# Cutting the first half of an output projection into pieces between attention steps, and splitting the first head's weights on another engine

## The chip, the core and the metric

The kernel runs on one core of a Trainium2 chip. TensorE (PE in the profile) multiplies matrices and transposes tiles; VectorE (DVE), ScalarE (ACT) and GpSimd (POOL) work element by element; transfers are issued by SyncE (SP) and by ScalarE. Each engine takes its instructions in the order in which they were built, and waits on semaphores for the others. The metric is the device time of one execution in microseconds. Before the change it is 2502.75 us, the median of three runs (2502.54 to 2502.87).

## The reference

Two transformer layers over 1024 tokens of width 1024, in float32. Layer 0 mixes tokens by differential attention (8 heads, each with two softmax maps whose difference weighs the values), layer 1 by latent attention (16 heads). After each stands a gated MLP with a causal convolution of width 3.

```python
def diff_attention(h, w_qkv, lq1, lk1, lq2, lk2, subln_g, w_o, lambda_init, cos, sin):
    qkv = h @ w_qkv
    ...
    def block(args):
        sc = jnp.einsum('bqhcd,bkhcd->bhcqk', qb, k).astype(jnp.float32) * scale
        p = masked_softmax(sc, chunk_mask(blk, s)[None, None, None])
        a = p[:, :, 0] - lam * p[:, :, 1]
        return jnp.einsum('bhqk,bkhe->bqhe', a.astype(v.dtype), v)
    ...
    o = rms_norm(o, subln_g) * (1.0 - lambda_init)
    return o.reshape(b, s, D_MODEL) @ w_o

for i in range(DEPTH):
    h = rms_norm(x, attn_norm_g[i])
    x = x + (diff_attention(h, ...) if i % 2 == 0 else mla_attention(h, ...))
    h = rms_norm(x, ffn_norm_g[i])
    x = x + conv_ffn(h, ...)
return rms_norm(x, final_norm_g)
```

## The kernel before, in words

**Float32 products in three passes.** Every operand of a matrix product is split into a rounded high part and the rest, the low part: `hi` (line 127, a cast on ScalarE) and `lo` (line 130, the source minus its high part, on VectorE or GpSimd). `mm3` (lines 119 to 121) then multiplies low by high, high by high and high by low into one accumulator in PSUM. A 128x512 accumulator over four blocks of 128 takes 12 matmuls, one over eight blocks takes 24.

**The PSUM banks.** `big()` gives one of two tiles of 1024 columns, named S; `bank("b")` one of three tiles of 512 columns, named b; `bank("u")` the one tile of 512 columns named u. A new accumulator in u can begin only when the last one has been read out.

**The start of layer 0.** Eight token tiles of 128 rows are fetched. `token_tile` takes each through a sum of squares (line 157, ScalarE), `root` (line 162 on VectorE, line 163 on GpSimd), the norm (line 349, VectorE, two operands in SBUF) and eight transposes on TensorE (line 182), whose results are split by ScalarE and VectorE into H. The projections of head 0 (`unit(0, which, half)`, which = 1 for k, 0 for q, 2 for v) multiply H by the head's weights; `split_w` splits those weights (slots s8 to s11), the low part on GpSimd. A k or q unit ends with `rope`: a copy of the accumulator (line 233, ScalarE), a shuffle of it (line 234, VectorE), and three steps on GpSimd (lines 235 to 237), then the splits into k (lines 430, 431) or into q (lines 127, 125 and, on GpSimd, 130). A v unit ends with a copy (line 417) and transposes of that copy.

**The head steps.** `steps` runs 32 steps of `DaStep` (eight heads, four steps each) in a software pipeline: scores of step t, transposes and product of step t-1, and the finish of step t-2; between them stand the projection units of the next head. In step t, `scores` fills two S tiles for each of two query blocks; DVE takes the row maximum, ScalarE the exponentials, GpSimd a scaling (line 149), DVE the difference of the two maps (line 1356). `turn` (line 249) transposes the result, `product` multiplies by v in bank b. Every second step ends with `finish`: two matmuls against ones (lines 1384, 1385), three ScalarE steps, one GpSimd step (line 173), three VectorE steps, and a store of 128x512 results to o_d in DRAM (line 1389, issued by SP).

**Output projection 0.** `project_first` computes, for the eight token tiles in the order 0, 4, 1, 5, 2, 6, 3, 7, the contribution of heads 0 to 3 and adds the input x: it loads o_d (line 449, SP), splits it into four pieces of slot s12 (high on ScalarE, low on GpSimd), multiplies, and adds to X in slots s8 to s11. The first four tiles accumulate in u, in two halves of 512 columns, with an addition for each half (line 473); the last four in S, with one addition of 1024 columns (line 478). `project_rest` does heads 4 to 7 in S, adds (line 554), stores x (line 555), normalises (line 515), forms sums on GpSimd (lines 492 to 499) and transposes them (line 182) for the MLP. The output projection of layer 1 uses the same two functions, with all tiles of the first half in S.

**What sets the order.** A list scheduler orders the instructions of each engine by its own estimate of time; only inside a region that is marked as manual (from `project_rest` to the end of each MLP) do PE and DVE instructions keep the order of the code among themselves. Instructions written ahead of the region may be set between those inside it. So a change in the code can move rows on every engine, and the order that results is fixed in the program.

Of the kernel before, what the change touches and what calls it, by code (L numbers as in the profile page):

```python
# [18 lines left out]
P = 128  # L19
S = 1024  # L20
D = 1024
NT = S // P
# [34 lines left out]
class Trunk:  # L57
# [220 lines left out]
    def steps(self, attend, units, prepare, n):  # L278


        steps = []
        for t in range(n + 2):
            now = before = None
            u = []
            if t < n:
                now = attend(t)
                steps.append(now)
                prepare(t)
                u = units(t)
# [12 lines left out]
            if now:  # L302
                now.weigh(1)
            if t >= 2:
                steps[t - 2].finish()


    def diff_attention(self, o_d, prefetch):
        nc, a = self.nc, self.a

        H = [[[self.at(f"s{4 * half + 2 * part + g}", [P, 4, 512], F32R) for g in range(2)] for half in range(2)] for part in range(2)]
# [18 lines left out]
            if h < DA_HEADS:  # L330
                raws[h, which] = self.fetch(a["da_wqkv"][h, which], D)

        def split_w(h, which):
            if h < DA_HEADS:
                raw = raws.pop((h, which))
                w = self.w([P, 2, D], F32R)
                self.hi(w[:, 0, :], raw)
                self.lo(w[:, 1, :], raw, w[:, 0, :], nc.gpsimd)
                heads[h]["w", which] = w[:, 0, :], w[:, 1, :]


# [12 lines left out]
        def unit(h, which, half):  # L354
            hd = heads[h]
            return self.da_unit(R, H, hd["w", which], which, half, hd, tab)

        xs = [fetch_x(0)]
        g = self.gain("s11", a["attn_norm_g"][0])
# [2 lines left out]
        xs += [fetch_x(3)]  # L362
        fetch_w(0, 0)
        nc.sync.dma_start(tab, a["rope_da"])
        split_w(0, 1)
        for i in range(4):
            token_tile(i, xs[i])
            if i == 1:
                self.load_constants()
        xs += [fetch_x(4), fetch_x(5), fetch_x(6)]  # L370
        fetch_w(0, 2)
        split_w(0, 0)
        self.run([unit(0, 1, 0)])
        split_w(0, 2)
        fetch_w(1, 1)
        self.run([unit(0, 0, 0)])
        for i in range(4, NT):
            if i + 3 < NT:
                xs += [fetch_x(i + 3)]
            token_tile(i, xs[i])  # L380
        self.run([unit(0, 2, 0)])

        def prepare(t):
            h, p = divmod(t, 4)
            if p == 0:
# [12 lines left out]
        def units(t):  # L398
            h, p = divmod(t, 4)
            todo = [[(h, 1, 1), (h, 2, 1)], [(h, 0, 1), (h + 1, 1, 0)], [(h + 1, 0, 0)], [(h + 1, 2, 0)]][p]  # L400
            return [unit(*u) for u in todo if u[0] < DA_HEADS]

        self.steps(lambda t: DaStep(self, R, *divmod(t, 4), heads, o_d), units, prepare, 4 * DA_HEADS)

    def da_unit(self, R, H, W, which, half, hd, tab):

        nc = self.nc
        acc = self.bank("u")
        for k in range(KD):
            wh, wl = (w[:, k * P : (k + 1) * P] for w in W)  # L410
            rh, rl = (H[part][half][k // 4][:, k % 4, :] for part in range(2))
            self.mm3(acc, wh, wl, rh, rl, k == 0, k == KD - 1)
            if k == 3:
                yield
        if which == 2:
            v = R.rope([P, 512])
            nc.scalar.copy(v, acc)
# [39 lines left out]

        return into

    def project_first(self, W, o_d, os, x_src, at, early):  # L460

        nc = self.nc
        X = [None] * NT
        for q, pair in enumerate(self.PAIRS):
            for i in pair:
                X[i] = at(q, i)
                nc.sync.dma_start(X[i], x_src[i * P : (i + 1) * P, :])
                into = self.project(i, range(0, 4), W, o_d, os, self.raw)
                if q < early:
                    for b in (0, 512):  # L470
                        y = self.bank("u")
                        into(y, b)
                        nc.vector.tensor_add(X[i][:, b : b + 512], X[i][:, b : b + 512], y)
                else:
                    y = self.big()
                    for b in (0, 512):
                        into(y[:, b : b + 512], b)
                    nc.vector.tensor_add(X[i], X[i], y)
        return X

    def project_rest(self, W, o_d, os, X, at, x_d, g, junk, places, nat, more):

# [704 lines left out]
    def mla_heads(self, cT, kT, v_d, o_d):  # L1187
# [85 lines left out]
        def units(t):  # L1273
            p, u = divmod(t, 8)

            at = (2, 3, 4, 5, 6, 7) if p == 0 else (0, 1, 3, 4, 5, 7)
            return [pair_units(p + 1)[i]() for i in range(6) if at[i] == u and p + 1 < pairs]

        def attend(t):

# [163 lines left out]
def kernel_body(tc, a, out):  # L1444
    with ExitStack() as ctx:
# [41 lines left out]

        W = []
        step, finish = prefetcher(a["da_w_o"], W, slots(*range(8)))
        k.diff_attention(o_d[0], step)  # L1490
        finish()
        first = {}
# [86 lines left out]
        heads.rest(step)  # L1579
        finish()  # L1580
        places = iter(units(2, 3, 4, 5, 12, 13, 10, 11))
        X = k.project_first(W, o_d[1], k.ring(*halves(0, 1, 2, 3)), x_d[1], lambda q, i: k.at(next(places), [P, D]), 0)
# [114 lines left out]
```

## Time and profile before

| | |
|---|---|
| median of three runs | 2502.75 us |
| the profiled execution | 2506.9 us |
| its span | 2505.1 us |
| TensorE busy | 2390.0 us, 95% of the span |
| VectorE, ScalarE, GpSimd busy | 1979.3, 1271.8, 725.4 us |
| mean granted TensorE clock | 0.988 |

A timeline row reads: start in the span, duration, engine, line, operation, tile written and tiles read, shape, count, and in brackets the idle time of the engine ahead of it with what ended it. A row of the table of stretches gives for each engine the busy time and the number of instructions, then the granted TensorE clock as a share of full speed, the DMA share and GB/s. A row of the list of waits gives the total, the number of times and the longest. Tile names are given without their numbers: s, u and h are slots in SBUF, S, b and u (as a matmul's output) the banks.

### The profile page before, as it was taken

How to read it: one execution, taken by the hardware profiler on the slowest of the kernel's cores; microseconds unless marked ns; L12 is line 12 of the kernel's file. 1: busy time of each engine (PE TensorE's matmuls, PEld its weight loads, DVE VectorE, ACT ScalarE, POOL GpSimd, SP SyncE). 2: the span in 40 equal slices, each digit the busy share in tenths (PEclk: the TensorE clock that was granted, in tenths of full speed). 3: DMA queues.
4: the chain of work that ended last, by engine and by line, in shares of the span. 5: the costliest groups of instructions: out<-in, count | busy, mean ns of one | idle time of the engine just before them, and what ended most of it. 6: DMA issues, size and time to landing. Idle time of an engine off the chain costs nothing.

```text
span 2505.1 us, 32665 instructions
## 1 busy us (share of the span) xinstructions
PE 2390.0 (95%) x11960; PEld 2015.0 (80%) x11960; DVE 1979.3 (79%) x3164; ACT 1271.8 (51%) x2323; POOL 725.4 (29%) x562
## 2 busy tenths in 40 slices
PE   6999999889999999999989899999999999999998
PEld 5787877778888888878878788888887888887887
DVE  6788888765788888889973787877368888888998
ACT  5566666643444444444443777777244444444444
POOL 5666666534300000000041566666350000000002
PEclk9999999989999999999999999999999999999999
DMA  4111111313122222454121211113322222227401
GB/s 148 35 46 35 36 41 43 109 58 124 65 79 85 85 84 85 151 192 145 57 107 43 80 37 39 39 55 98 107 97 76 93 76 84 86 83 272 154 20 76
DMA packets 95104, 214.44 MB, mean 86 GB/s; under 512 B 8640, under 2 KB 33856, under 8 KB 94784
## 3 DMA queue, kind: packets, MB, share of 16 engines
q1 hardware_dynamic: 86048, 185.09, 22.3%
q10 hardware_dynamic: 8896, 27.27, 3.0%
q8 instruction: 94, 1.54, 0.2%
q14 instruction: 66, 0.54, 0.1%
HBM read 159.89 MB, written 52.43 MB: 85 GB/s over the span
## 4 chain that ended last, share of the span: by engine, by line
PE 75%; DVE 13%; ACT 4%; issue 3%; DMA 3%; POOL 2%; SPq 0%; DVEq 0%; ACTq 0%; POOLq 0%
PE S L119 12%; PE S L120 12%; PE S L121 12%; PE b L119 7%; PE b L120 7%; PE b L121 7%; PE u L119 3%; PE u L120 3%; PE u L121 3%; PE b L249 2%; DVE s L130 2%; PE b L182 1%; PE u L1433 1%; PE u L1432 1%; DVE u L1356 1%
## 5 line engine op out<-in xcount | busy, mean ns | idle before, releaser
L119 PE MATMUL S<-s,u 128*128 128x512 f32 (+1 forms) x752 | 285.8, 380 | 5.6 <-DVE u L769 3.8
L121 PE MATMUL S<-s,u 128*128 128x512 f32 (+1 forms) x752 | 284.1, 378 | 0.0
L120 PE MATMUL S<-s,u 128*128 128x512 f32 (+1 forms) x752 | 284.1, 378 | 0.0
L127 ACT CAST u<-h 128x512 fp32r<-128x512 f32 (+2 forms) x210 | 126.4, 620 | 284.4 <-DVE h L631 255.9
L163 POOL TENSOR_TENSOR st<-st,mhalf 128x1 f32<-128x1 f32 x56 | 41.3, 740 | 717.5 <-DVE st L162 709.9
L119 PE MATMUL b<-s,u 128*128 128x512 f32 x588 | 231.5, 394 | 0.5
L120 PE MATMUL b<-s,u 128*128 128x512 f32 x588 | 229.6, 390 | 0.0
L121 PE MATMUL b<-s,u 128*128 128x512 f32 x588 | 229.5, 390 | 0.0
L679 DVE SCALAR_TENSOR_TENSOR u<-u,conv,u 128x1023 f32<-128x1023 f32 (+1 forms) x176 | 225.0, 1278 | 1.6 <-ACT u L675 1.6
L149 POOL TENSOR_TENSOR u<-u,st 128x384 f32<-128x384 f32 (+7 forms) x160 | 171.6, 1080 | 136.0 <-DVE st L1418 102.9
L119 PE MATMUL u<-s,s 128*128 128x512 f32 x432 | 177.6, 411 | 17.9 <-DVE h L234 12.8
L130 POOL TENSOR_TENSOR u<-s,u 128x960 fp32r<-128x960 f32 (+1 forms) x5 | 12.8, 2576 | 598.8 <-DVE s L130 587.6
L130 DVE TENSOR_TENSOR u<-b,u 128x512 fp32r<-128x512 f32 (+1 forms) x256 | 158.1, 631 | 32.6 <-ACT u L127 30.7
L127 ACT CAST s<-u 128x512 fp32r<-128x512 f32 (+2 forms) x195 | 128.1, 692 | 100.6 <-PE u L121 32.5
L121 PE MATMUL u<-s,s 128*128 128x512 f32 x432 | 173.7, 402 | 0.0
L120 PE MATMUL u<-s,s 128*128 128x512 f32 x432 | 173.0, 400 | 0.0
L119 PEld LDWEIGHTS S<-s,u 128*128 128x128 f32 x752 | 141.4, 188 | 34.2 <-issue 4.4
L121 PEld LDWEIGHTS S<-s,u 128*128 128x128 f32 x752 | 141.3, 188 | 26.3
L120 PEld LDWEIGHTS S<-s,u 128*128 128x128 f32 x752 | 141.4, 188 | 26.0
L127 ACT CAST u<-b 128x512 fp32r<-128x512 f32 (+1 forms) x256 | 133.7, 551 | 51.6 <-PE b L249 43.0
L249 PE MATMUL b<-ident,u 128*128 128x128 f32 x864 | 137.3, 279 | 13.6 <-DVE u L130 5.7
L682 ACT ACTIVATE u<-u 128x1024 f32<-128x1024 f32 x44 | 46.7, 1062 | 199.1 <-DVE u L679 199.1
(260 smaller groups left out, 6885.4 us busy)
## 6 DMA issues: line engine op xcount, KB each, us to landing
u<-in_ffn_up SPq DMA_DIRECT2D x88, 512.0 KB, 3.9
g_d<-u ACTq DMA_DIRECT2D x44, 512.0 KB, 2.6
u<-in_ffn_down SPq DMA_DIRECT2D x66, 256.0 KB, 5.2
u<-g_d SPq DMA_DIRECT2D x62, 256.0 KB, 4.3
s<-in_da_wqkv SPq DMA_DIRECT2D x24, 512.0 KB, 3.6
x_d<-u SPq DMA_DIRECT2D x16, 512.0 KB, 2.9
s<-x_d SPq DMA_DIRECT2D x8, 1024.0 KB, 11.0
u<-o_d SPq DMA_DIRECT2D x24, 256.0 KB, 2.8
```

What stands on the lines that cost most here:

```text
L119: mm(out, lh, rl, start=first, stop=False, skip_group_check=onto)
L120: mm(out, lh, rh, start=False, stop=False, skip_group_check=onto)
L121: mm(out, ll, rh, start=False, stop=last, skip_group_check=onto)
L127: self.nc.scalar.copy(out, src)
L130: (eng or self.nc.vector).tensor_sub(out, src, hi.bitcast(F32))
L149: self.nc.gpsimd.tensor_mul(x, x, s.to_broadcast(list(x.shape)))
L163: nc.gpsimd.tensor_tensor(r, s, self.mhalf, ALU.pow)
L182: self.nc.tensor.transpose(ps[:, k * P : (k + 1) * P], src[:, k * P : (k + 1) * P], self.ident)
L249: self.nc.tensor.transpose(ps[:, j * P : (j + 1) * P], probs[t][:, k : k + P], self.ident)
L679: nc.vector.scalar_tensor_tensor(t[half][:, back:], u[half][:, : S - back], w, t[half][:, back:], ALU.mult, ALU.add)
L682: nc.scalar.activation(t[0], t[0], AF.Silu)
L1356: nc.vector.scalar_tensor_tensor(p0, p1, w, p0, ALU.mult, ALU.add)
```

## The change

It has three parts.

1. **The start.** The low parts of head 0's three weight tiles are computed on VectorE instead of GpSimd. The first split (`split_w(0, 1)`) comes after two token tiles; the fifth token tile is taken right after the k unit and the sixth before the v unit. The q unit `unit(0, 0, 0)` accumulates in a b bank instead of u. `load_constants` comes later.
2. **The end of attention 0.** `project_first` becomes a generator of pieces. Its pieces are handed to the steps 30 to 33 as units, two tiles to each, so that they stand between the last head's steps in the code; the o_d tiles are loaded into h8 and h9 instead of s13; all eight tiles accumulate in u, a half of 512 columns at a time. The prefetch of the projection's weights begins one step earlier.
3. **Output projection 1** uses the same pieces with bank b: two halves of 512 columns and two additions a tile, instead of S and one addition.

```diff
@@ steps
-            u = []
             if t < n:
                 now = attend(t)
                 steps.append(now)
                 prepare(t)
-                u = units(t)
+            u = units(t)
+            if now:
                 now.scores(0)
@@ diff_attention
-        def split_w(h, which):
+        def split_w(h, which, eng=nc.gpsimd):
...
-                self.lo(w[:, 1, :], raw, w[:, 0, :], nc.gpsimd)
+                self.lo(w[:, 1, :], raw, w[:, 0, :], eng)
...
-        split_w(0, 1)
         for i in range(4):
+            if i == 2:
+                split_w(0, 1, nc.vector)
             token_tile(i, xs[i])
-            if i == 1:
-                self.load_constants()
...
-        split_w(0, 0)
+        split_w(0, 0, nc.vector)
         self.run([unit(0, 1, 0)])
-        split_w(0, 2)
+        token_tile(4, xs[4])
+        split_w(0, 2, nc.vector)
         fetch_w(1, 1)
-        self.run([unit(0, 0, 0)])
-        for i in range(4, NT):
-            if i + 3 < NT:
-                xs += [fetch_x(i + 3)]
+        self.run([unit(0, 0, 0, "b")])
+        self.load_constants()
+        for i in range(5, NT):
+            if i + 2 < NT:
+                xs += [fetch_x(i + 2)]
             token_tile(i, xs[i])
-        self.run([unit(0, 2, 0)])
+            if i == 5:
+                self.run([unit(0, 2, 0)])
...
-            if h + 1 == DA_HEADS:
+            if t >= 4 * DA_HEADS - 5:
                 prefetch()
...
         def units(t):
             h, p = divmod(t, 4)
+            if t >= 4 * DA_HEADS - 2:
+                if not ready:
+                    ready.append(project(self.ring("h8", "h9")))
+                return [next(ready[0]) for _ in range(2)]
@@ project_first
+        def tile(i, into):
+            for b in (0, 512):
+                y = bank()
+                into(y, b)
+                nc.vector.tensor_add(X[i][:, b : b + 512], X[i][:, b : b + 512], y)
+                yield
...
-                into = self.project(i, range(0, 4), W, o_d, os, self.raw)
-                if q < early:
-                    for b in (0, 512):
-                        y = self.bank("u")
-                        into(y, b)
-                        nc.vector.tensor_add(X[i][:, b : b + 512], X[i][:, b : b + 512], y)
-                else:
-                    y = self.big()
-                    for b in (0, 512):
-                        into(y[:, b : b + 512], b)
-                    nc.vector.tensor_add(X[i], X[i], y)
-        return X
+                yield tile(i, self.project(i, range(0, 4), W, o_d, os, raw))
@@ kernel_body
-        X = k.project_first(W, o_d[0], k.ring(*k.cut("s12", 512)), a["x"], at, 2)
+        k.diff_attention(o_d[0], step, lambda raw: k.project_first(
+            W, o_d[0], k.ring(*k.cut("s12", 512)), raw, a["x"], at, X, lambda: k.bank("u")))
+        finish()
...
+        for tile in k.project_first(W, o_d[1], k.ring(*halves(0, 1, 2, 3)), k.raw, x_d[1], lambda q, i: k.at(next(places), [P, D]), X, k.bank):
+            k.run([tile])
```

Every engine does the same arithmetic apart from the three low parts (GpSimd to VectorE) and the additions: the four additions of 1024 columns in projection 0 and the eight in projection 1 become twice as many of 512. How the instructions move is shown at four places; numbers behind a name tell tiles of one name apart.

VectorE in the first 20 us, from the norm of the third token tile on (line 349 writes u_62; s_54 holds raw weights, s_74 and s_88 the split weights of the k and the q unit). Before:

```order
L349 SCALAR_TENSOR_TENSOR u_62_161<-u_62_161,st_80_231,s_60_157 128x1024
L130 TENSOR_TENSOR s_49_141<-b_199,s_45_137 128x4x128
L162 TENSOR_SCALAR st_84_250<-st_84_250 128x1
L130 TENSOR_TENSOR s_50_142<-b_206,s_46_138 128x4x128
L349 SCALAR_TENSOR_TENSOR u_63_164<-u_63_164,st_85_252,s_60_157 128x1024
```

After:

```order
L349 SCALAR_TENSOR_TENSOR u_62_161<-u_62_161,st_77_216,s_60_157 128x1024
L130 TENSOR_TENSOR s_74_210<-s_54_146,s_74_210 128x1024
L130 TENSOR_TENSOR s_49_141<-b_196,s_45_137 128x4x128
L162 TENSOR_SCALAR st_81_235<-st_81_235 128x1
L130 TENSOR_TENSOR s_50_142<-b_203,s_46_138 128x4x128
L130 TENSOR_TENSOR s_88_262<-s_54_146,s_88_262 128x1024
L130 TENSOR_TENSOR s_49_141<-b_220,s_45_137 128x4x128
L349 SCALAR_TENSOR_TENSOR u_63_164<-u_63_164,st_82_237,s_60_157 128x1024
```

Two splits of 128x1024 now stand between the norms of the third and the fourth tile.

GpSimd in the last head's third step (line 149 scales the softmax, u_958 and u_960 are the same slot u8; s_1039 and s_973 are the pieces of s12 for the projection; h_57 and h_58 the low parts of the next q). Before:

```order
L149 TENSOR_TENSOR u_950_4707<-u_950_4707,st_948_4699 128x384
L130 TENSOR_TENSOR h_943_4681<-h_941_4679,h_942_4680 128x512
L149 TENSOR_TENSOR u_958_4744<-u_958_4744,st_956_4736 128x512
L130 TENSOR_TENSOR h_57_149<-h_959_4759,u_961_4766 64x512
L130 TENSOR_TENSOR h_58_150<-h_959_4759,u_961_4766 64x512
L130 TENSOR_TENSOR s_1039_5093<-s_54_146,s_1039_5093 128x512 x2
```

After:

```order
L149 TENSOR_TENSOR u_952_4715<-u_952_4715,st_950_4707 128x384
L130 TENSOR_TENSOR s_973_4817<-h_975_4820,s_973_4817 128x512
L130 TENSOR_TENSOR s_973_4817<-h_976_4825,s_973_4817 128x512
L149 TENSOR_TENSOR u_960_4752<-u_960_4752,st_958_4744 128x512
L130 TENSOR_TENSOR h_945_4689<-h_943_4687,h_944_4688 128x512
L130 TENSOR_TENSOR h_57_149<-h_961_4767,u_963_4774 64x512
L130 TENSOR_TENSOR h_58_150<-h_961_4767,u_963_4774 64x512
```

The two low parts for the projection moved ahead of a softmax scaling, of the low part that the finish needs, and of the next q.

TensorE ahead of the first transposes of a sum in output projection 0 (line 182 reads h_1085 or h_1097, the sum that GpSimd forms at line 492, now 496, from tile 4's norm). Before:

```order
L119 MATMUL S_5496<-s_1038_5090,h_1083_5469 128x512
L120 MATMUL S_5496<-s_1038_5090,h_1083_5469 128x512
L121 MATMUL S_5496<-s_1038_5090,h_1084_5470 128x512
L182 MATMUL b_5511<-ident,h_1085_5486 128x128 x4
L119 MATMUL S_5496<-s_993_4894,h_1083_5469 128x512
```

After:

```order
L119 MATMUL u_5334<-s_948_4701,s_973_4817 128x512
L120 MATMUL u_5334<-s_948_4701,s_973_4817 128x512
L121 MATMUL u_5334<-s_948_4701,s_973_4817 128x512
L182 MATMUL b_5527<-ident,h_1097_5502 128x128 x4
L119 MATMUL S_5512<-s_971_4809,h_1095_5485 128x512
```

The last two accumulators of the first half (24 matmuls into u_5320 and u_5334) now stand right ahead of these transposes.

VectorE in the same stretch (lines 554, now 558: the final addition of a tile; 515, now 519: its norm; u_1072 and u_1084 are tile 4). Before:

```order
L554 TENSOR_TENSOR u_1072_5428<-s_1040_5094,S_5396 128x1024
L162 TENSOR_SCALAR st_1073_5431<-st_1073_5431 128x1
L130 TENSOR_TENSOR s_1077_5450<-b_5451,s_1076_5449 128x4x128
L130 TENSOR_TENSOR s_1080_5459<-b_5460,s_1079_5458 128x4x128
L515 SCALAR_TENSOR_TENSOR u_1072_5428<-u_1072_5428,st_1074_5433,u_1056_5346 128x1024
```

After:

```order
L558 TENSOR_TENSOR u_1084_5444<-s_974_4818,S_5412 128x1024
L162 TENSOR_SCALAR st_1085_5447<-st_1085_5447 128x1
L476 TENSOR_TENSOR s_1057_5281<-s_1057_5281,u_5292 128x512
L476 TENSOR_TENSOR s_1057_5281<-s_1057_5281,u_5306 128x512
L476 TENSOR_TENSOR s_1057_5281<-s_1057_5281,u_5320 128x512
L130 TENSOR_TENSOR s_1089_5466<-b_5467,s_1088_5465 128x4x128
L476 TENSOR_TENSOR s_1057_5281<-s_1057_5281,u_5334 128x512
L130 TENSOR_TENSOR s_1092_5475<-b_5476,s_1091_5474 128x4x128
L519 SCALAR_TENSOR_TENSOR u_1084_5444<-u_1084_5444,st_1086_5449,u_1068_5362 128x1024
```

The norm of tile 4 now stands behind the additions that read the last four accumulators of the first half.

More of the change, by code (lines that the diff above doesn't have):

```diff
@@ L305, in steps, with diff_attention @@
                 steps[t - 2].finish()
-    def diff_attention(self, o_d, prefetch):
+    def diff_attention(self, o_d, prefetch, project):
         nc, a = self.nc, self.a
@@ L352, in token_tile, with unit @@
                 self.turn_blocks(x[:, kg * 512 : (kg + 1) * 512], lambda part: H[part][i // 4][kg][:, :, s])
-        def unit(h, which, half):
+        def unit(h, which, half, acc="u"):
             hd = heads[h]
-            return self.da_unit(R, H, hd["w", which], which, half, hd, tab)
+            return self.da_unit(R, H, hd["w", which], which, half, hd, tab, acc)
         xs = [fetch_x(0)]
@@ L399, in units, with da_unit @@
             h, p = divmod(t, 4)
+            if t >= 4 * DA_HEADS - 2:
+                if not ready:
+                    ready.append(project(self.ring("h8", "h9")))
+                return [next(ready[0]) for _ in range(2)]
             todo = [[(h, 1, 1), (h, 2, 1)], [(h, 0, 1), (h + 1, 1, 0)], [(h + 1, 0, 0)], [(h + 1, 2, 0)]][p]
             return [unit(*u) for u in todo if u[0] < DA_HEADS]
+        ready = []
         self.steps(lambda t: DaStep(self, R, *divmod(t, 4), heads, o_d), units, prepare, 4 * DA_HEADS)
-    def da_unit(self, R, H, W, which, half, hd, tab):
+    def da_unit(self, R, H, W, which, half, hd, tab, acc):
         nc = self.nc
-        acc = self.bank("u")
+        acc = self.bank(acc)
         for k in range(KD):
@@ L458, in project, with project_first @@
         return into
-    def project_first(self, W, o_d, os, x_src, at, early):
+    def project_first(self, W, o_d, os, raw, x_src, at, X, bank):
         nc = self.nc
-        X = [None] * NT
+        def tile(i, into):
[4 more added lines that the diff above has]
+                yield
         for q, pair in enumerate(self.PAIRS):
@@ L1276, in units @@
             at = (2, 3, 4, 5, 6, 7) if p == 0 else (0, 1, 3, 4, 5, 7)
-            return [pair_units(p + 1)[i]() for i in range(6) if at[i] == u and p + 1 < pairs]
+            return [pair_units(p + 1)[i]() for i in range(6) if p + 1 < pairs and at[i] == u]
         def attend(t):
@@ L1489, in kernel_body @@
         step, finish = prefetcher(a["da_w_o"], W, slots(*range(8)))
-        k.diff_attention(o_d[0], step)
-        finish()
-        first = {}
+        first, X = {}, [None] * NT
         def at(q, i):
@@ L1581, in kernel_body @@
         places = iter(units(2, 3, 4, 5, 12, 13, 10, 11))
-        X = k.project_first(W, o_d[1], k.ring(*halves(0, 1, 2, 3)), x_d[1], lambda q, i: k.at(next(places), [P, D]), 0)
+        X = [None] * NT
+        for tile in k.project_first(W, o_d[1], k.ring(*halves(0, 1, 2, 3)), k.raw, x_d[1], lambda q, i: k.at(next(places), [P, D]), X, k.bank):
+            k.run([tile])
         pl = SimpleNamespace(
```

## The prediction, on record before the result

> **What bounds the kernel now.** I read the busy times first, then the stretches by stage, then the waits of TensorE in the stretches that the change touches.
>
> ```profile
> PE 2390.0 (95%) x11960; PEld 2015.0 (80%) x11960; DVE 1979.3 (79%) x3164; ACT 1271.8 (51%) x2323; POOL 725.4 (29%) x562
> 0.00:75.00 75.00, 53.68 (x248) 43.91 (x248) 51.90 (x77) 38.00 (x72) 40.45 (x42) 0.98 0.38 138
> 425.00:560.00 135.00, 117.63 (x597) 97.33 (x596) 98.18 (x162) 77.80 (x152) 68.96 (x49) 0.92 0.25 80
> 690.00:1200.00 510.00, 504.31 (x2219) 415.86 (x2219) 440.14 (x612) 221.53 (x338) 0.00 (x0) 1.00 0.32 111
> ```
>
> TensorE is the bound: in the MLP (690 to 1200) it works 504 of 510 us, 504.31 / 2219 = 0.227 us a matmul at clock 1.00. The change removes no matmul, so it can win only where TensorE stands still or has a low clock: 21 us of the first 75, and 17 of the 135 up to 560, where the clock is also 0.92. Outside the start, the last head's steps with output projection 0, and output projection 1, the order of rows is unchanged.
>
> The profiled execution took 2506.9 us, 4.15 above the median of 2502.75; I make the sum in its rows and carry the difference to the median.
>
> **Part 1, the start.**
>
> ```profile
> 6.67 1.29 DVE L349 SCALAR_TENSOR_TENSOR u<-u,st,s 128x1024 f32<-128x1024 f32 x1 [0.75 <-POOL st L163]
> 12.41 2.35 POOL L130 TENSOR_TENSOR s<-s,s 128x1024 fp32r<-128x1024 f32 x1
> 12.47 3.36 DVE L349 SCALAR_TENSOR_TENSOR u<-u,st,s 128x1024 f32<-128x1024 f32 x1
> 17.16 3.36 DVE L349 SCALAR_TENSOR_TENSOR u<-u,st,s 128x1024 f32<-128x1024 f32 x1
> L130 DVE TENSOR_TENSOR s<-s,s x2: 1200/1206/1212, 496.0 to 507.1; 128x1024 fp32r<-128x1024 f32 x2
> 23.15 0.79 PE L119 MATMUL u<-s,s 128*128 128x512 f32 x1 [0.55 <-DVE s L130]
> 33.32 0.50 PE L119 MATMUL u<-s,s 128*128 128x512 f32 x1 [1.38 <-DVE h L234]
> 38.90 1.48 PE L182 MATMUL b<-ident,u 128*128 128x128 f32 x12
> 43.38 0.53 PE L119 MATMUL u<-s,s 128*128 128x512 f32 x1 [3.00 <-DVE h L234]
> 43.00:53.00 10.00, 9.62 (x45) 0.83 0.02 6
> 52.78 0.48 PE L119 MATMUL u<-s,s 128*128 128x512 f32 x1
> 67.33 0.66 PE L182 MATMUL b<-ident,h 128*128 128x128 f32 x4 [1.61 <-ACT h L417]
> PE u L119 <- DVE h L234: 12.8, 10, 3.0
> ```
>
> A norm takes 1.29 us alone, and 3.36 while GpSimd splits weights (12.41 beside 12.47). With the splits on VectorE two norms get back 2 x 2.07; ahead of the first unit VectorE then does two splits of 1.20 and the fifth tile's norm of 1.28. So the first projection matmul moves from 23.15 to about 23.4: no gain here, none lost.
>
> The gain is behind it. TensorE waited 1.38 (33.32) and 3.00 (43.38) for the shuffle that reads the single u bank, and then ran ten microseconds at 0.83 (9.62 x 0.17 = 1.6 lost). With q in a b bank no unit waits for the one before. Walked forward: k unit from 23.4 to 31.1 with four transposes in it; q, 24 matmuls in 5.58 (33.32 to 38.90), to 36.6; eight transposes; v from 37.5 to 43.0; a wait of 0.75 for its copy; scores from 45.2; the next unit at 48.4, against 52.78. That is -4.4: the 6.0 of the three items less 0.25 at the first unit, the 0.75 and 0.6 for the rest. The 1.61 at 67.33 falls to about 0.6, since the copy it waits for stands earlier on ScalarE: -1.0. Sum **-5.4**; bounds -7.8 (6.0 + 1.61 all gained) and -2.0 (the waits alone, halved, if q's chain of rope takes their place).
>
> **Part 2a, the last head's steps.**
>
> ```profile
> 502.76 0.69 PE L249 MATMUL b<-ident,u 128*128 128x128 f32 x2 [2.83 <-DVE u L1356]
> 505.81 0.79 PE L119 MATMUL u<-s,s 128*128 128x512 f32 x1 [2.36 <-ACT s L127]
> 508.82 0.58 PE L119 MATMUL b<-u,u 128*128 128x256 f32 x1 [1.78 <-DVE u L130]
> 539.48 0.50 PE L119 MATMUL u<-s,s 128*128 128x512 f32 x1 [0.56 <-DVE s L473]
> 505.00:517.00 12.00, 9.40 (x34) 0.59 0.24 68
> 511.01 0.62 ACT L127 CAST s<-s 128x512 fp32r<-128x512 f32 x1 [5.25 <-DMA s<-o_d]
> 511.18 2.52 POOL L130 TENSOR_TENSOR s<-s,s 128x512 fp32r<-128x512 f32 x2
> ```
>
> Already before, matmuls of the projection stood among these steps, but late: the first cast of o_d starts at 511.01, after its load. TensorE lost 2.83 + 2.36 + 1.78 = 7.0 in waits at 500 to 509 and, at clock 0.59, 9.40 x 0.41 = 3.9 more up to 517: 10.9 together, 11.4 with the 0.56. With o_d loaded a step earlier, the first group of 12 matmuls (12 x 0.227 = 2.7) stands in the waits, and none that is left reaches the 3.00 that lowered the clock at 43.38: -2.7 - 3.9. Against it, two low parts for the projection (2.52 / 2 = 1.26 each on GpSimd, 511.18) now stand ahead of a softmax scaling (line 149) and of the low part for the finish; line 1356 and the transposes wait behind that scaling: +2.5. What the pieces issue besides moves with them: the o_d and x loads on SP, one cast (0.62) on ScalarE for each piece of o_d, and the weights' splits, 1.20 each on VectorE, a step earlier. I take nothing for these: the transfers use 0.25 of the DMA engines from 425 to 560, ScalarE is busy 78 of those 135 us, and VectorE's total of 98 does not change; if a cast stands ahead of the exponentials, it costs 0.62 a time, which the upper bound of 0 takes in. The loads wait on SP only for the two slots h8 and h9, and no load of a head's weights is behind them. The 0.56 stays, once, wherever two groups meet in the u bank. Sum **-4.1**; bounds -11.4 (every loss goes) and 0 (the low parts cost what the group fills, the clock still drops).
>
> **Part 2b, from the last product to the first sums.** The 19 matmuls (4.3 us) that stood late in S now stand ahead, in u; that only moves them. New are the waits:
>
> ```profile
> 538.74 0.69 DVE L473 TENSOR_TENSOR s<-s,u 128x512 f32<-128x512 f32 x1 [1.32 <-PE u L121]
> 556.60 5.72 SPq L449 DMA_DIRECT2D u<-o_d  x2
> 559.95 0.62 ACT L127 CAST h<-u 128x512 fp32r<-128x512 f32 x1 [1.78 <-DMA u<-o_d]
> 563.45 0.40 PE L1384 MATMUL b<-h,ones 128*128 128x512 f32 x1
> 573.07 5.20 SPq L449 DMA_DIRECT2D u<-o_d  x2
> 575.89 0.62 ACT L127 CAST h<-u 128x512 fp32r<-128x512 f32 x1 [9.71 <-DMA u<-o_d]
> 590.44 1.27 DVE L515 SCALAR_TENSOR_TENSOR u<-u,st,u 128x1024 f32<-128x1024 f32 x1
> 591.79 1.30 POOL L492 TENSOR_TENSOR h<-u,u 128x512 f32<-128x512 f32 x1 [3.00 <-PE S L121]
> 594.31 0.60 PE L182 MATMUL b<-ident,h 128*128 128x128 f32 x4
> 595.56 0.69 DVE L130 TENSOR_TENSOR s<-b,s 128x512 fp32r<-128x512 f32 x1 [1.13 <-ACT s L127]
> 600.24 1.03 PE L182 MATMUL b<-ident,u 128*128 128x128 f32 x8
> ```
>
> - The first tile of `project_rest` needs its o_d in a slot that the last product frees; load to cast is 3.35 (556.60 to 559.95) and the cast 0.62, so it is ready 4.1 after that product. Less work is left to fill that, 2.8: **+1.3**.
> - The last head's finish, its store, load (573.07) and cast (575.89) arrive about 11.3 after the ones matmul, 12.4 to 13.1 before (563.45 to 575.89 + 0.62); TensorE now gets there in 10.5: **+0.8**.
> - The last two groups of the first half stand back to back in the one u bank: 0.69 (538.74) and a semaphore, **+0.8**.
> - The transposes of the first sum (594.31) come right behind these groups. Their sum waits, on VectorE in order, for the last addition (0.74), a low part (0.65), tile 4's norm (1.28), then GpSimd's 1.30: about **+4.05**. Before, S groups stood there.
>
> Together +7.0, bounds 0 (the estimates of arrival are each about 1 to 4 us, and other groups fill) and +9. A gap of 4 us brings in the clock, of which the trace shows both kinds:
>
> ```profile
> 1072.50 0.50 PE L119 MATMUL b<-s,s 128*128 128x512 f32 x1 [3.06 <-DVE s L996]
> 1072.00:1075.00 3.00, 2.50 (x11) 1.00 1.09 378
> ```
>
> After 3.06 the clock stayed at 1.00, after 3.00 (43.38) it fell. For 4.05 I take the fall and its 1.6; bounds 0 and the 3.9 of 505 to 517. The Trainium skill ("TensorE: Matmul & The Clock Gate", "What's actually happening") says that the clock halves only after a whole idle window of about 3.4 us, counted in windows that run on freely; 43.38 fell after less, so the trace does not bear out that length. By that rule a gap of 4.05 need not hold a whole window; the term would be 0 and the time 2500.6, by an estimate from the page.
>
> **Part 3, output projection 1.**
>
> ```profile
> 1750.00:1800.00 50.00, 50.00 (x237) 1.00 0.28 90
> 1759.75 1.22 DVE L478 TENSOR_TENSOR u<-u,S 128x1024 f32<-128x1024 f32 x1 [0.86 <-PE S L121]
> ```
>
> TensorE is busy 50 of 50 us here. Two additions of 0.69 replace one of 1.22, +0.16 a tile on VectorE, against 24 x 0.227 = 5.4 us of matmuls a tile; three b banks are enough for groups of 2.7. **+0.2**, bounds -0.1 and +1 (one bank awaited once).
>
> **The sum.** -5.4 - 4.1 + 7.0 + 1.6 + 0.2 = -0.7. On the median: about **2502.1 us**.
>
> **The rivals.**
> 1. *The stall around 500 to 517 goes whole* (faster). For it: the first waits are 2.83, 2.36 and 1.78, and 2.7 us of ready matmuls in each of three gaps would cover all; the clock would stay. Against: GpSimd's two low parts stand ahead of the scaling. It gives 7.3 more than the sum: 2494.8.
> 2. *The norm's delay repeats at the next transposes* (slower). At 600.24, 5.9 behind 594.31, eight transposes need the next sum; its chain is an addition of 1024 columns (1.22 in a row of part 3), a norm (1.27) and GpSimd's sums of 1.30, and by my count ends 4.5 after. The margin is some 1.5 us of work on VectorE and GpSimd; if what is put off by the four additions exceeds it, a second gap of 4.05 with 1.6 of low clock follows: +5.7, 2507.8.
> 3. *The start's gain is not had* (slower): q's own rope chain and its splits come later than the scores, so that TensorE waits there for what it no longer waits for at the bank; only the 67.33 wait changes. -5.4 becomes 0: 2507.5. For it: L234 had ended ten waits of TensorE, up to 3.0 long; against: three b banks are free there.
>
> **How the numbers follow.** My sum 0.46, rival 1 0.28, rival 2 0.16, rival 3 0.10. A time within 0.2% (5 us) of before is about what a measurement tells from no change. Faster by more: most of rival 1 (0.22) and 0.10 of my own case, whose terms have bounds of several us: 0.32. Slower by more: half of rivals 2 and 3 (0.14) and 0.09 of my own: 0.23. The same: 0.45. My case alone reaches from 2497 to 2507; 2493.5 and 2509.5 take in rivals 1 to 3 with about half of their own spread.
>
> **What would show it right or wrong.** In the changed profile: the unit at 52.78 starts near 48.4 with no wait for L234 ahead of q or v, and the norms take 1.3; the end of the last product of head 7 comes near 548, not 556.5, apart from the start's shift; TensorE waits about 4 us ahead of the first L182 of h in projection 0, with a clock below 1.00 behind it; 1750 to 1800 (shifted) is full. I am wrong in size if the clock between 500 and 520 is near 1.00 throughout (rival 1), if two gaps of 4 us stand in 575 to 610 (rival 2), or if a wait of over 2 us stands at the first scores (rival 3).

## The result, and the profile after

| | |
|---|---|
| before, beside it | 2502.64 us, median of 6 runs (2500.03 to 2504.68) |
| changed | 2511.51 us, median of 6 runs (2506.39 to 2514.87) |
| ratio, 95% interval | 1.0035 (1.0022 to 1.0048) |
| the profiled execution, its span | 2512.24 us, 2510.5 us |

The change made the kernel 8.9 us slower. A second comparison, below, gives 7.0. Forecast were 2502.1 us, 0.7 below before, and at most 2509.5.

The busy times and the stretches of the changed kernel, with the columns as before (busy time and number for PE, PEld, DVE, ACT and POOL, then the clock):

```profile
PE 2394.5 (95%) x11960; PEld 2016.6 (80%) x11960; DVE 1975.6 (79%) x3179; ACT 1271.2 (51%) x2323; POOL 714.9 (28%) x559
0.00:75.00 75.00, 57.86 (x269) 46.96 (x270) 45.33 (x82) 39.49 (x75) 37.42 (x42) 1.00 0.37 138
425.00:560.00 135.00, 118.38 (x584) 96.24 (x582) 99.02 (x157) 77.73 (x146) 66.74 (x50) 0.94 0.27 84
560.00:690.00 130.00, 117.35 (x626) 99.96 (x627) 74.45 (x98) 47.58 (x79) 45.84 (x39) 0.96 0.25 81
690.00:1200.00 510.00, 505.56 (x2216) 417.38 (x2215) 438.85 (x608) 220.17 (x337) 0.00 (x0) 0.99 0.33 113
```

Up to 75 us TensorE did more (57.86 us busy instead of 53.68); from 560 to 690 it did 626 matmuls instead of 683. The loss stands there. The waits of TensorE from 490 on, from the timeline of the changed kernel:

```profile
47.91 0.50 PE L119 MATMUL u<-s,s 128*128 128x512 f32 x1 [1.15 <-DVE s L130]
496.10 0.69 PE L249 MATMUL b<-ident,u 128*128 128x128 f32 x2 [2.09 <-DVE u L1360]
498.01 0.80 PE L121 MATMUL u<-s,s 128*128 128x512 f32 x1 [1.22 <-POOL s L130]
504.12 0.39 PE L119 MATMUL b<-u,u 128*128 128x256 f32 x1 [1.92 <-DVE u L130]
548.33 0.50 PE L119 MATMUL S<-s,h 128*128 128x512 f32 x1 [0.35 <-ACT h L127]
562.84 0.69 PE L119 MATMUL S<-s,h 128*128 128x512 f32 x1 [2.85 <-ACT h L127]
590.90 0.50 PE L119 MATMUL u<-s,s 128*128 128x512 f32 x1 [0.78 <-DVE s L476]
597.84 1.12 PE L182 MATMUL b<-ident,h 128*128 128x128 f32 x4 [3.92 <-POOL h L496]
```

The first row is the unit that stood at 52.78. The last four rows are the four waits that part 2b forecast; the profile before has none in these places. Behind two of them the clock is low, here in windows of TensorE alone (busy time, number, clock, DMA share, GB/s), and in the last steps it is little higher than before (third row changed, the row of its own before):

```profile
562.00:567.00 5.00, 4.16 (x11) 0.66 0.51 150
597.80:605.00 7.20, 7.16 (x21) 0.57 0.18 73
485.00:525.00 40.00, 32.84 (x163) 0.87 0.27 86
```

```profile
485.00:525.00 40.00, 30.91 (x154) 0.83 0.36 119
```

4.16 x 0.34 + 7.16 x 0.43 = 4.5 us are lost to the clock behind the two waits. In the last steps the 40 us hold stretches at full clock too. The low stretches by themselves are one before and two in the changed kernel:

```profile
501.30:514.95 13.65, 8.04 (x28) 0.50 0.21 62
```

```profile
494.70:501.50 6.80, 4.18 (x10) 0.50 0.26 72
505.00:508.40 3.40, 3.40 (x13) 0.51 0.02 5
```

8.04 x 0.50 = 4.0 us were lost there before, and 4.18 x 0.50 + 3.40 x 0.49 = 3.8 are lost now.

To place gains and losses, TensorE's matmuls are numbered as they stand in the trace, and the time of one number is compared between two kernels. Up to number 2205 lies the start with the heads before the last steps, up to 2900 the last steps and projection 0. The table gives by how many us each stretch got longer than before, in the one profiled execution of each; drops of the clock in one execution and not in the other are in it (1.7 at 139 us in the first column, for example). For e7, which has 27 matmuls more, the same work is compared.

| kernel | to 2205 | 2205 to 2900 | 2900 to 11000 | median, ratio to before |
|---|---|---|---|---|
| changed | -6.7 | +13.1 | +1.1 | 2511.5, 1.0035 |
| e1 start only | -7.0 | +1.8 | -0.8 | 2500.0, 0.9983 |
| e2 start and pieces | -7.6 | +9.8 | -1.4 | 2509.1, 1.0019 |
| e4 last tiles in S | -6.9 | +8.7 | -13.3 | 2493.3, 0.9953 |
| e5 half after the steps | -4.0 | -0.6 | -14.6 | 2484.7, 0.9928 |
| e6 before, one pair in u | -0.8 | -1.4 | -13.6 | 2488.9, 0.9949 |
| e7 gap filled | -7.5 | +12.0 | -12.1 | 2497.0, 0.9980 |
| e8 low parts on VectorE | -7.6 | +8.3 | +2.7 | 2508.3, 1.0020 |
| e9 q casts on ScalarE | -7.6 | +12.1 | +0.8 | 2506.8, 1.0017 |
| e10 start, all in S | -4.8 | +6.2 | -12.0 | 2490.7, 0.9947 |
| e11 changed again | -7.7 | +9.7 | -0.4 | 2511.2, 1.0025 |

### The profile page after: what moved, and what is told of

It is laid out like the page before. It is cut to its first block, busy times and chain, and to the rows that moved or that the text cites. A ratio compares the mean times of both kernels' runs of the same rounds, so it can differ in the third digit from the quotient of the medians.

```text
span 2510.5 us, 32676 instructions
## 1 busy us (share of the span) xinstructions
PE 2394.5 (95%) x11960; PEld 2016.6 (80%) x11960; DVE 1975.6 (79%) x3179; ACT 1271.2 (51%) x2323; POOL 714.9 (28%) x559
## 3 DMA queue, kind: packets, MB, share of 16 engines
q8 instruction: 94, 1.54, 0.3%
## 4 chain that ended last, share of the span: by engine, by line
PE 75%; DVE 13%; ACT 4%; DMA 3%; issue 2%; POOL 2%; SPq 0%; DVEq 0%; ACTq 0%; POOLq 0%
PE S L119 11%; PE S L120 11%; PE S L121 11%; PE b L119 8%; PE b L121 8%; PE b L120 8%; PE u L119 3%; PE u L120 3%; PE u L121 3%; PE b L249 2%; DVE s L130 2%; PE b L182 1%; PE u L1437 1%; PE u L1436 1%; DVE u L1360 1%
## 5 line engine op out<-in xcount | busy, mean ns | idle before, releaser
L149 POOL TENSOR_TENSOR u<-u,st 128x384 f32<-128x384 f32 (+7 forms) x160 | 170.9, 1075 | 138.8 <-DVE st L1422 103.9
L119 PE MATMUL u<-s,s 128*128 128x512 f32 x456 | 187.1, 410 | 12.8 <-DVE h L234 9.0
L121 PE MATMUL u<-s,s 128*128 128x512 f32 x456 | 183.1, 402 | 1.2 <-POOL s L130 1.2
L120 PE MATMUL u<-s,s 128*128 128x512 f32 x456 | 182.2, 399 | 0.0
```

The source lines that it names most:

```text
L119: mm(out, lh, rl, start=first, stop=False, skip_group_check=onto)
L120: mm(out, lh, rh, start=False, stop=False, skip_group_check=onto)
L121: mm(out, ll, rh, start=False, stop=last, skip_group_check=onto)
L149: self.nc.gpsimd.tensor_mul(x, x, s.to_broadcast(list(x.shape)))
```

## The experiments

**The parts apart (e1, e2, e3).** The first takes only the diff's hunks on `split_w`, `token_tile`, `unit` and `da_unit`; the second all but output projection 1; the third projection 1 alone.

> The start of the changed kernel on the kernel before, nothing else. If the loss sits wholly in the pieces of projection 0, this is faster by what the start's trace shows, -5.0 us by TensorE's 250th matmul: about 2497.5 us. If the start's gain is given back in the following steps, it is within 1.5 us of before.

> The changed kernel with output projection 1 as before (S, one addition a tile). If the pieces of projection 0 carry the loss, the time is that of the changed kernel within 1 us, about 2511, and TensorE loses some 13 us between its 2205th and its 2800th matmul as in the changed kernel. If projection 1 carries a part, it is lower by that part (2 to 6 us).

> Only output projection 1 in pieces with bank b. The prediction's +0.2 gives 2502.8. If the doubled additions delay the norms there as in projection 0, some 3 to 6 us more.

Measured: e1 0.9983 (0.9974 to 0.9992), -4.3 us; e2 1.0019 (1.0011 to 1.0028), +4.8; e3 1.0001 (0.9992 to 1.0010), +0.3 (-2 to +2.5). The start gains, projection 1 cannot be told from nothing, and the pieces of projection 0 cost e2 - e1 = 9.1 us. In e1's trace the 250th matmul is 5.2 earlier. For e2 the forecast was the changed kernel's time within 1 us and some 13 us lost behind the 2205th matmul: the trace has 9.8, like e11's 9.7, and the ratio lies below the changed kernel's (1.0035, and 1.0025 in e11), though the intervals overlap. That difference is not placed.

**Where the last accumulators stand (e4).** `early` is 2 for projection 0 and 4, so without effect, for projection 1.

```diff
+            if q >= early:
+                y = self.big()
+                for b in (0, 512):
+                    into(y[:, b : b + 512], b)
+                nc.vector.tensor_add(X[i], X[i], y)
+                yield
+                return
```

> The changed kernel, but the last four tiles of projection 0's first half accumulate in S with one addition of 1024 columns each, as before the change. Theory: the wait of 3.92 at the first transposes of a sum comes from the two accumulators and the additions that stand right ahead of them; here they stand further ahead, so this wait and the 0.78 go (and with them the low clock at 597 to 604, 3.7 us); but all first-half matmuls now stand ahead of the last ones matmul, so the wait for the last head's o_d grows from 2.85 to about 6. Sum about -4 to -6 against the changed kernel: 2506. Rival: the norm and GpSimd's subtraction are late by themselves (tile 4's x comes late); then a wait of 3 to 4 us stays at these transposes and the time is 2511 or more.

The only wait of TensorE between 525 and 625 us of this run:

```profile
579.39 0.80 PE L119 MATMUL S<-s,h 128*128 128x512 f32 x1 [7.17 <-ACT h L127]
```

The 3.92 and the 0.78 are gone, and the wait for the last head's o_d has grown from 2.85 to 7.17 (6 was expected). So the wait at the first transposes does come from the accumulators and additions ahead of it, and the other from too little work between the ones matmul and the load. From 2205 to 2900 it loses 8.7 instead of 13.1, as forecast. The total was 13 us under the forecast: the order of layer 1, far from the edit, had changed with it, and that stretch is 13.3 shorter. Nobody had aimed at that. It was the next question.

**Is it the order of layer 1 (e6)?** One number in the kernel before:

```diff
-        X = k.project_first(W, o_d[0], k.ring(*k.cut("s12", 512)), a["x"], at, 2)
+        X = k.project_first(W, o_d[0], k.ring(*k.cut("s12", 512)), a["x"], at, 1)
```

> The kernel before, with one number changed: two tiles of projection 0's first half accumulate in u instead of four. The order in layer 1 changes with it to the one of the run with the last tiles in S. Theory: that order of layer 1 is worth about -12 us by itself, between matmuls 6500 and 8500; projection 0 moves by less than 2. Total about 2491. Rival: that run's 13 us came from the clock or from where it stood in time; then 2503 to 2505.

0.9949 (0.9936 to 0.9961), 2488.9 against 2503.7: the theory holds. 13.6 us come from layer 1. TensorE's transposes of line 249 there, by groups, before (first) and in e6 (second; count, busy and mean, then idle time ahead of them):

```profile
L249 PE MATMUL b<-ident,u 128*128 128x128 f32 x542 | 85.3, 277 | 8.2 <-DVE u L130 5.7 <-DVE s L130 1.5 <-DVE S L1410 0.5
```

```profile
L249 PE MATMUL b<-ident,u 128*128 128x128 f32 x545 | 83.1, 275 | 1.8 <-DVE u L130 0.9 <-DVE s L130 0.5 <-DVE h L1230 0.2
```

These transposes wait 6.4 us less, mostly for low parts on VectorE. Some 1.7 more were a drop of the clock that e6 does not have in layer 1 (0.97 before from 1680 to 1740). What makes the rest of the 13.6 is not shown.

**Half of the pieces (e5, e12).** As e4, but the steps 32 and 33 take no pieces, and the rest of them is run behind the steps:

```diff
+            if t >= 4 * DA_HEADS:
+                return []
...
+        for tile in left:
+            k.run([tile])
```

> The changed kernel, but only the first four tiles of projection 0's first half stand in the steps 30 and 31; the last four come behind the steps, in S, with one addition each. 48 matmuls (10.9 us) stand now between the last ones matmul and the first use of the loaded o_d. Theory: the waits of 2.85 (7.17 with the last tiles in S but ahead of the ones), 0.78 and 3.92 all go with their low clock, so TensorE's 2800th matmul, against before, stands at -7 to -9 us instead of +6.5. The order in layer 1 is the other one that the run with the last tiles in S had, which gave it 13 us between matmuls 6500 and 8500: the total is then about 2483. Rival: the 13 us came from something else than the order of layer 1 (the clock), then about 2495.

> The version with half of the pieces between the steps, with output projection 1 as before (S, one addition a tile). Theory: projection 1 in pieces costs nothing that can be measured (+0.2 by the prediction, 0.3 by its own run), so 2484 to 2486. Rival: its doubled additions cost 2 us or more, which the run of projection 1 alone was too coarse to show (its interval reaches from -2 to +2.5); then 2483 or less.

e5: 0.9928 (0.9915 to 0.9942), 2484.7 us, 19 us under its before; it is the fastest. TensorE waits for nothing between 545 and 605, and its 2800th matmul is 4.6 earlier than before: less than the 7 to 9 forecast, since 4.0 were gained at the start in this execution and 6.7 to 7.7 in most others with that start. Compare the row of the changed kernel from 560 to 690, 117.35 busy at 0.96:

```profile
560.00:690.00 130.00, 124.86 (x683) 1.00 0.28 92
```

e12, with projection 1 as before, is 0.9925 (0.9911 to 0.9939), 2486.1: no difference from e5.

**Do the pieces between the steps bring anything (e10)?** The start, and all eight tiles behind the steps in S (`early` 0 in the code before).

> The start of the changed kernel, and projection 0's first half behind the steps as before, with all eight tiles in S. The order of layer 1 is the faster one. Theory: the start (-4.3) and that order (-14.8) add up and the pieces between the steps bring nothing by themselves: 2484 to 2486 against a before of 2503.7, as the version with half of the pieces. Rival: the pieces in the steps 30 and 31 bring 2 us or more, and this one is slower by that: 2487 or more.

0.9947 (0.9934 to 0.9961), 2490.7: the rival holds, by 6 us against e5. Without matmuls of the projection in the stall, as TensorE's close waits around 490 to 505 us are called here, one wait there is

```profile
504.01 0.58 PE L119 MATMUL b<-u,u 128*128 128x256 f32 x1 [5.36 <-DVE u L130]
```

and the stretch is 6.2 longer. But the kernel before had such matmuls in its last steps already. e1, which keeps its way, is 2.4 longer than e5 in this stretch (+1.8 and -0.6), of which 1.3 are two short waits for an addition at 562 to 564. So matmuls of the projection in that place are worth some 6 us, and the change's way of placing them at most some 2 of it more than the old one. The medians give it nothing: e1's -4.3 and e6's -14.8 add up to -19.1, and e5 is -19.0. So what e5 gains is the start and the other order of layer 1; the pieces, at their best place, cost nothing and bring nothing that these runs can tell.

**What the gap costs through the clock (e7).** 27 transposes that read what the last addition writes, in the gap of 3.92:

```diff
+                if q == 0 and x_d is self.warm:
+                    for n in range(3):
+                        ps = self.bank()
+                        for k in range(9):
+                            b = slice(k % 4 * P, k % 4 * P + P)
+                            nc.tensor.transpose(ps[:, b], X[7][:, 512:640], self.ident)
                 turns(("T1", q))
...
+        k.warm = x_d[0]
```

> The changed kernel with 27 more transposes of 128x128 (some 3.1 us) on TensorE between the last accumulator of the first half and the first transposes of a sum; they read what the last addition writes, so that they stand in the gap of 3.92, and what they write is not used. Theory: the gap becomes a wait of about 0.8 and 3.1 us of work, the clock stays at 1.00 at 597 to 604, and the 2800th matmul comes 1.7 to 3.5 us earlier than in the changed kernel; by the prediction's size of a drop 1.6. Rival: the low clock there comes from the load that follows, not from the gap, and stays. The order of layer 1 is the other one here too, so the total is read up to matmul 5000 only.

```profile
594.73 3.17 PE L543 MATMUL b<-ident,s 128*128 128x128 f32 x27 [0.78 <-DVE s L476]
597.89 0.66 PE L182 MATMUL b<-ident,h 128*128 128x128 f32 x4
597.80:605.00 7.20, 7.20 (x40) 1.00 0.23 89
```

The transposes that waited stand at 597.89, where they stood (597.84), but the clock behind them is 1.00 instead of 0.57, and 40 matmuls go in 7.2 us instead of 21. The work that was the 2800th matmul comes 2.9 us earlier against the time ahead of the gap (0.9 of it goes again at a wait for a later sum, at 611.5). In the traces of the changed kernel, e2, e8, e9 and e11 the wait of 3.92 stands, and in each the clock falls there. So the low clock came from the gap; its price in this comparison was 2.9 us, where 1.6 were forecast. The total of e7, 0.9980 (0.9969 to 0.9990), has the faster order of layer 1 in it and says nothing about the gap.

**What makes the stall at 490 to 505 (e8, e9).** In the changed kernel's stall VectorE had no gap, and its weight split took 2.30 us beside a low part on GpSimd, 1.21 before (507.08, where VectorE's started first):

```profile
501.29 2.30 DVE L130 TENSOR_TENSOR s<-s,s 128x1024 fp32r<-128x1024 f32 x1
500.92 1.59 POOL L130 TENSOR_TENSOR h<-h,h 128x512 fp32r<-128x512 f32 x1 [0.36 <-DVE h L125]
```

```profile
507.08 1.21 DVE L130 TENSOR_TENSOR s<-s,s 128x1024 fp32r<-128x1024 f32 x1
```

e8 gives the low parts of the first two tiles to VectorE (`self.lo(ol, o, oh, eng or nc.gpsimd)`), e9 takes q's casts from it:

```diff
-                self.hi(qh[other, c], r[own], nc.vector)
+                self.hi(qh[other, c], r[own], None if last else nc.vector)
```

> The changed kernel with the low parts of the projection's first two tiles on VectorE instead of GpSimd. Theory: in the stall at 492 to 505 VectorE's casts of the next q (2.88 instead of 1.83) and its weight split (2.30 instead of 1.21) were slowed by GpSimd's work beside them; without the two low parts of 1.35 on GpSimd the casts take about 1.9 again, GpSimd's later steps come 2.7 earlier, and VectorE has 1.3 more to do: the stall shortens by 1 to 2 us. Rival: the order on VectorE alone (casts ahead of the difference of line 1356, now 1360) makes the stall; then it does not shorten, or grows by the 1.3.

> The changed kernel with the two casts of 64x512 of the last head's second q on ScalarE, where they took 2.88 us of VectorE at 496.8; TensorE's order is the same row by row. Theory: in the stall at 489 to 505 VectorE has no gap, and its sum of work sets when TensorE goes on; with 2.9 us less the product at 504.1 starts 1.5 to 2.9 us earlier, and the total falls by about as much. Rival: GpSimd (its scalings and low parts, also without a gap) sets the stall; then the product moves by less than 0.7 us.

```profile
503.11 0.80 PE L1332 MATMUL S<-u,h 128*128 128x512 f32 x1 [3.34 <-POOL h L130]
```

In e8 the stall did not shorten: its last wait (row above) is now for GpSimd's low part of the next q, and the 2400th matmul is 2.0 later against the 2205th than in the changed kernel. That theory fell; its 1.0020 (1.0010 to 1.0031) is not told apart from the changed kernel's. In e9 VectorE got a gap of 1.39, and the product that waited came 7.4 us behind the transposes instead of 8.0 (and 8.3 in e11):

```profile
502.58 0.58 PE L119 MATMUL b<-u,u 128*128 128x256 f32 x1 [0.90 <-DVE u L130]
```

0.6 to 0.9 for 2.9 us less work, less than the forecast (1.5 to 2.9) and near the bound of its rival (0.7): VectorE's sum is a part of what sets the stall, not all of it. Besides the gap, two of VectorE's steps there took longer (a cast of line 125 1.54 instead of 1.15, line 1360 1.39 instead of 0.60). Which chain through VectorE and GpSimd sets the stall, stays open. The time of e9, 1.0017 (1.0008 to 1.0026), is not told apart from the changed kernel's beside it, 1.0025.

**The changed kernel once more (e11).**

> The changed kernel once more, beside the others on the same chip: 2508 to 2513. In the profile the waits stand where they stood (about 2.9, 0.8 and 3.9 between 560 and 600), since the order is fixed; the stretches of low clock behind them differ in number and length, 0 to 6.8 us each. If they are the same as before to the microsecond, the clock follows from the waits alone.

2511.15 us against 2504.11, 1.0025 (1.0016 to 1.0035). Its profiled execution took 2506.4 us, the first one 2512.2, with nearly the same waits (2.49, 0.78 and 3.92 against 2.85, 0.78 and 3.92) and less low clock (the last row holds its one low stretch in the last steps):

```profile
485.00:525.00 40.00, 32.72 (x166) 0.91 0.28 93
559.00:564.00 5.00, 4.04 (x11) 0.66 0.50 162
594.00:606.00 12.00, 11.06 (x51) 0.86 0.41 136
495.30:502.20 6.90, 4.79 (x12) 0.51 0.26 77
```

Behind the 3.92 the loss is 11.06 x 0.14 = 1.5 us here, 3.1 in the first. So the clock does not follow from the waits alone: the same wait costs one stretch of low clock in one execution and two in another. The runs of the changed kernel spread over 8.5 us.

## Why the prediction was wrong

| step | forecast | measured |
|---|---|---|
| part 1, the start | -5.4 | -5.0 in the trace, -4.3 by e1 |
| part 2a, the last steps | -4.1 | -0.5; -1.9 in e11 |
| part 2b, the waits | +7.0 | +7.9; +7.5 in e11 |
| part 2b, the clock behind them | +1.6 | +4.5; +2.9 in e11 |
| part 3, projection 1 | +0.2 | +0.3, within 2.5 (e3) |

- **Part 1** was right in place and size. The next unit stands at 47.91 (48.4 forecast), behind a wait of 1.15 for a split on VectorE that the forecast lacks. The window from 43 to 53, which was at 0.83, is at 1.00, and the norms take 1.28.
- **Part 2a is the step that failed most.** "None that is left reaches the 3.00 that lowered the clock at 43.38: -2.7 - 3.9": the clock did fall again, behind waits of 2.09, 1.22 and 1.92 that stand close together. By the rows of the low stretches, 4.0 us lost became 3.8, so 0.2 came back and not 3.9; in e11 4.79 x 0.49 = 2.3 are lost, so 1.7 came back. It is no accident of one execution: in e2, e4, e5, e7, e9 and e11 the longest wait of the stall is 2.03 to 2.41, and the clock falls in each. The whole term was measured from the end of the heads' earlier steps to that of the last product, 467.07 to 544.82 with 355 matmuls, against 473.75 to 556.49 with 375 before: 77.75 + 20 x 0.227 - 82.74 = -0.5. Less the clock's 0.2, -0.3 is left, where -2.7 + 2.5 = -0.2 was forecast; e11 leaves -0.2. So what failed is the clock in this sum, and not the work moved. The group of 12 stands in the stall, as forecast, but the stall grew from 9.2 us (499.64 to 508.82) to 11.1 (493.04 to 504.12), so that the 2.7 and the 2.5 that were to be set against each other did nearly cancel. The clock's 3.9 was counted as gained because each wait was held against 3.00 by itself.
- **Part 2b's waits** came out almost to the size: 0.35 for 1.3, 2.85 for 0.8, 0.78 for 0.8, 3.92 for 4.05. The second was mis-sized because I took the last head's way from the ones matmul through DRAM to the cast to be shorter than before, 11.3; in the changed kernel it took 548.90 to 562.84, 13.9. One of its steps ran beside a low part for the pieces and took 1.70 instead of 0.69:

```profile
552.93 1.70 DVE L174 SCALAR_TENSOR_TENSOR h<-h,h 128x512 f32<-128x512 f32 x1
552.79 1.28 POOL L130 TENSOR_TENSOR s<-h,s 128x512 fp32r<-128x512 f32 x1
```

- **The clock behind the waits** was mis-sized twice: there are two drops, since the 2.85 brings its own, and one drop may last two stretches (e7: 2.9 for the gap of 3.92). The Trainium skill ("TensorE: Matmul & The Clock Gate", "What's actually happening") has windows of 3.4 us that run on freely, and asks for an idle one. That the windows run on freely agrees with e11. Taken as a gap of at least 3.4 us, the idle window does not agree: gaps of 2.49 and 2.85 sufficed. The time of 2500.6 that the prediction worked out from that rule is 11 us too low.
- **The rivals.** The stall did not go (rival 1). No second gap of 4 us stands behind the first (rival 2), and the start's gain was had (rival 3). With 2a at its upper bound of 0 and the clock at its bound of 3.9 the prediction's own sum is 2502.75 - 5.4 + 0 + 7.0 + 3.9 + 0.2 = 2508.5, and the waits came out 0.9 longer; the clock's 4.5 lies above its bound of 3.9 besides. The range ended at 2509.5: it left no room for two terms at their bad ends in one kernel, though both hang on the same clock. Two slips in the working change nothing: half of rivals 2 and 3 is 0.13 and not 0.14, and the terms without the clock's 1.6 give 2500.5 and not 2500.6.

The measured terms sum to -5.0 - 0.5 + 7.9 + 4.5 + 0.3 = +7.2, and with e11's profile, where the 250th matmul is 4.6 earlier, to -4.6 - 1.9 + 7.5 + 2.9 + 0.3 = +4.2; the medians say 8.9 and 7.0. The profiled executions themselves took 5.3 more and 0.5 less than the profiled one before (2506.9). The single executions differ by the clock in places far from the change, so the sums are no closer than that, and some 2 to 3 us of the medians are not placed.

## What to carry to other kernels

Work that fills a wait is gained only if the waiting chain runs no slower beside it, and if it is not missed later: the matmuls that went forward had covered a way through DRAM of 13 us, and the additions of the pieces left behind stood on VectorE right ahead of the norm that the next transposes need. With half of them left where they covered the load, the loss was gone (e5). In this kernel a gap on TensorE of 2.5 us or more cost its own length and, in most executions, some 1.5 to 3 us of low clock; waits of some 2 us that stood close together brought the low clock as well. Price both, and look at the order of the whole program after an edit, not only around it: one number in layer 0 was worth 13.6 us in layer 1.

## What was not expected of the hardware

The same wait, in the same order, lowered the clock in some executions and not in others. The one for line 996 (now 1000) took 3.06 before, and the clock stayed at 1.00 from 1072 to 1075; in the changed kernel it took 3.24:

```profile
1079.34 0.79 PE L119 MATMUL b<-s,s 128*128 128x512 f32 x1 [3.24 <-DVE s L1000]
1075.00:1090.00 15.00, 11.76 (x40) 0.77 0.73 269
```

A clock of 0.77 over these 15 us means some 11.76 x 0.23 = 2.7 us lost, without any change in this place. Single executions of one kernel differ by 3 to 9 us here, in the same order of instructions, and the mean granted clock goes with it: of the six runs of the changed kernel, the shortest (2506.4 us) had 0.990 and the longest (2514.9) 0.985. So such drops are likely most of that spread; that they are all of it is not shown.
